# Mixer C of a hybrid encoder: its diagonal blocks moved by ScalarE's block copies, with four unread TensorE products for the first direction

## The chip, the cores and the metric

The kernel runs on one core of one Trainium2 chip. The metric is device time in microseconds (us), the median of several executions. The core's engines each run a queue of their own in order and wait for one another on semaphores: TensorE (PE, with its weight loads PEld), VectorE (DVE), ScalarE (ACT), GpSimd (POOL), and SyncE (SP), which issues most DMAs.

## What is computed

The reference is two encoder layers on 256 tokens of width 1024, in float32. Each layer projects the input once into the columns of four mixers, merges their gated outputs, and then applies a feed-forward block (layer 0) or a top-2-of-8 expert block (layer 1):

```python
for layer in range(DEPTH):                       # DEPTH = 2
    p = split_columns(x @ w_in[layer])
    y_a, y_b, y_c, y_d = mlstm(p), dilated_attention(p), deltanet_branch(p), window_attention(p)
    mix = (sum of sigmoid(gate_i) * (y_i @ w_branch_i)) @ w_out
    x = layer_norm(alpha * x + mix)
    x = layer_norm(alpha * x + (swiglu(x) or moe_swiglu(x)))
```

The change lies in mixer C, the gated DeltaNet, which runs over the sequence in both directions. For each direction and each chunk it solves a triangular system:

```python
decay = exp(where(incl, gc[i] - gc[j], -inf))
a_strict = where(strict, (k_beta @ k.T) * decay, 0.0)
sol = triangular_solve(a_strict, rhs, lower=True, unit_diagonal=True)
```

## The kernel before

A float32 product is done as three products of halves: ScalarE casts a weight to its high half (`wh<-raw`, L261), VectorE subtracts to get the low half (`wl<-raw,wh`, L264), and PE multiplies high by high, high by low and low by high into one PSUM bank. The names that PE's rows show for them are `mm<-wh,xh`, `mm<-wh,xl` and `mm<-wl,xh`. These projections of weight tiles are what PE does most of the time. In them the columns of a product are 256, 264 or 512.

In a layer's mixing stage the four mixers are generators. Between weight tiles `advance(n)` lets each of them emit a step, ahead of the projections' own instructions by a priority offset of 56. A list scheduler then orders each engine's queue by these priorities and by what is ready, so that taking an instruction out in one place moves others. Products of the mixers stand as `mx` in PE's rows, and each `mx` or `mm` tile is a bank from one of two rings of four.

Mixer C (`mix_c`) has two chunk pairs `t` and two directions `d`, 0 and 1. `systems(t)` computes the triangular systems `U` (tile `cU`, 128 partitions x 4 heads x 128). `leaves(d)` inverts their 32 x 32 diagonal blocks for one direction. It first gathers the blocks into `cYZ`: VectorE multiplies `U` by a block mask (`cum`, L132), adds up the four column groups (L878), copies the sum three more times (L880) and transposes it (L881). POOL starts `cX` as an identity. Then come 31 elimination steps on VectorE, two small instructions each (`cXt`, `cX`). The result is transposed to `cWc` (L900) and spread back over a block-diagonal tile `cW` by another masked multiply (L132), whose transpose is `cV` (L905). `unit(d, t)` combines the 32 x 32 blocks on PE, beginning with `mx<-cW,cU` products. `leaves` runs once for each direction in each of the two layers.

Rows of the sections below also name tiles of other mixers: `bp` (probabilities of mixer B's attention, evacuated by ScalarE), `bk` (its keys), `aw` (mixer A's weights) and `cS` (mixer C's state). `warm(n)` issues `n` products of an identity whose result nobody reads; the kernel before calls it outside the mixing stage.

Of the kernel before, what the change touches and what calls it, by code (L numbers as in the profile page):

```python
# [12 lines left out]
OP = mybir.AluOpType  # L13
AX = mybir.AxisListType
PSUM = bass.MemoryType.PSUM

P = 128
# [100 lines left out]
class Encoder:  # L118
# [41 lines left out]
        self.last_mm = self.nc.tensor.matmul(o, l, r, start=start, stop=stop, skip_group_check=True)  # L160
        return self.last_mm

    def warm(self, n):

        with self.tc.issue_after(self.last_mm.ins):
            o = self.bmm()
            for _ in range(n):
                self.mm(o[:], self.c["identb"], self.c["mbb"][:, :512])

# [573 lines left out]
    def mix_c(self):  # L743
        mp, nc, c = self.mp, self.nc, self.c
# [27 lines left out]
        after = mp.tile([P, 2, P], F32R, name="cafter")  # L772
# [3 lines left out]
        o = self.bmx()  # L776
# [14 lines left out]
        o = self.bmx()  # L791
# [8 lines left out]
        for k in (1, 0):  # L800
            o = self.bmx()
            for t in range(2):
                x = mp.tile([P, 4, 64], F32, name="crx", tag="t1", bufs=4)
# [6 lines left out]
        o = self.bmx()  # L810
# [7 lines left out]
        o = self.bmx()  # L818
# [15 lines left out]
        r3 = lambda x: x[:].rearrange("p (h i) -> p h i", i=P)  # L834
        U, at, V, W = {}, {}, {}, {}
# [31 lines left out]
        def leaves(d):  # L867


            yz = self.m8("cYZ")  # L870
            y, z = yz[:, :1024], yz[:, 1024:]
            yv = y.rearrange("p (i x t h) -> p i x t h", x=4, t=2, h=4)
            k32 = c["blk32"][:, None, :, None].to_broadcast([P, 4, 4, 32])
            for t in range(2):
                m = self.t2("cum", "cs")
                mv = m[:].rearrange("p (h k i) -> p h k i", k=4, i=32)
                self.tt(mv, U[d, t].rearrange("p h (k i) -> p h k i", i=32), k32, OP.mult)
                nc.vector.tensor_reduce(yv[:, :, 0, t, :].rearrange("p i h -> p h i"), mv.rearrange("p h k i -> p h i k"), AX.X, OP.add)  # L878
            y4 = y.rearrange("p (i x m) -> p i x m", x=4, m=8)
            nc.vector.tensor_copy(y4[:, :, 1:4], y4[:, :, 0:1].to_broadcast([P, 32, 3, 8]))  # L880
            nc.vector.transpose(z, y)  # L881
            zv = z.rearrange("p (i j) -> p i j", j=32)
            x = mp.tile([P, 8, 32], F32, name="cX", bufs=1)
            nc.gpsimd.tensor_copy(x[:], c["own32b"].rearrange("p (q r) -> p q r", q=8))
            tmp = mp.tile([P, 8, 32], F32, name="cXt", bufs=1)
            yield
            for n in range(31):
                i = 31 - n if d else n
                rows = slice(0, i) if d else slice(i + 1, 32)
                cs = slice(i // 4, 8) if d else slice(0, i // 4 + 1)  # L890
                sh = [P, cs.stop - cs.start, rows.stop - rows.start]
                f = zv[:, rows, i][:, None].to_broadcast(sh)
                pv = x[:, cs, i:i + 1].to_broadcast(sh)
                tv = tmp[:, cs, rows]
                self.tt(tv, f, pv, OP.mult)
                self.tt(x[:, cs, rows], x[:, cs, rows], tv, OP.subtract)
                if n % 3 == 2:
                    yield
            wc = mp.tile([P, 256], F32, name="cWc", bufs=1)
            nc.vector.transpose(wc[:], x[:].rearrange("p q r -> p (q r)"))  # L900
            wcv = wc[:].rearrange("p (c t h) -> p t h c", t=2, h=4)
            for t in range(2):
                w, vv = self.t2("cW", "cW"), self.t2("cV", "cV")
                self.tt(w[:].rearrange("p (h k c) -> p h k c", k=4, c=32), wcv[:, t][:, :, None, :].to_broadcast([P, 4, 4, 32]), k32, OP.mult)
                nc.vector.transpose(vv[:], w[:])  # L905
                W[d, t], V[d, t] = r3(w), r3(vv)
            yield
# [86 lines left out]
        for d in range(2):  # L994
            yield from leaves(d)
            both = [unit(d, t) for t in (d, 1 - d)]
            for _ in range(3):
                for q in both:
                    next(q)
                    yield  # L1000
# [683 lines left out]
```

## Time and profile before

| | |
|---|---|
| median of 3 timed runs | 1400.27 us (1399.23 to 1401.48) |
| the profiled execution | 1396.19 us, span of the trace 1394.3 us |
| mean granted TensorE clock | 0.988 of full speed |
| PE busy | 1334.3 us, 96% of the span |
| DVE busy | 1077.3 us, 77% |
| ACT busy | 744.8 us, 53% |
| POOL busy | 144.1 us, 10% |
| chain that ended last, by engine | PE 80%, DVE 12%, issue 3%, ACT 2%, DMA 2% |

The span is the profiled execution seen by the hardware profiler, from its first to its last instruction; the time of that execution is a little longer. A busy share says how long an engine was at work, not whether anybody waited for it. What an engine waited for is in the table of waits and in brackets behind a row of the timeline, where the idle time just before the row stands with the instruction that ended it. The granted clock is that of TensorE in the stretch, as a share of full speed; its two levels are 1.2 and 2.4 GHz.

### The profile page before, as it was taken

Reading aid. Unit: us, or ns where it says so; the run is one execution under the profiler, and the core shown is the slowest. Engines: PE = TensorE matmul, PEld = TensorE weight load, DVE = VectorE, ACT = ScalarE, POOL = GpSimd, SP = SyncE. Lnnn points to the kernel's source line nnn. Section 1 sums busy time; section 2 is a strip of 40 time slices with the busy share of each in tenths; the row PEclk is TensorE's granted clock in tenths of the full one; section 3 lists DMA queues with packets and bytes.
Section 4 is the critical chain, followed back from the end, with each engine's and each line's share of the span. In section 5 each row is a group of like instructions: output and inputs, shape, how many; then the busy total and the mean of one; then the engine's idle time right before and its main releaser. Section 6 shows DMA issues by size and latency. Waiting matters only on the chain.

```text
span 1394.3 us, 23092 instructions
## 1 busy us (share of the span) xinstructions
PE 1334.3 (96%) x8736; PEld 1152.2 (83%) x8740; DVE 1077.3 (77%) x1880; ACT 744.8 (53%) x1102; POOL 144.1 (10%) x118
## 2 busy tenths in 40 slices
PE   8999999999999999999989999998899999999994
PEld 7877879999789998887688899986777878877873
DVE  6979876775785554777888489579988888888887
ACT  5535443464364443354434446436777678676773
POOL 1000200023100000100020002220111111111110
PEclk9999999999999999999999999999999999999998
DMA  7632422595596563243252238744989989989981
GB/s 247 183 99 76 147 61 82 154 337 163 177 298 183 187 190 103 85 127 102 61 171 85 73 111 288 244 146 167 358 303 357 332 317 324 359 305 343 369 301 71
DMA packets 155751, 281.90 MB, mean 202 GB/s; under 512 B 11120, under 2 KB 58480, under 8 KB 155632
## 3 DMA queue, kind: packets, MB, share of 16 engines
q1 hardware_dynamic: 153136, 273.54, 58.8%
q10 hardware_dynamic: 1152, 4.19, 0.9%
q0 software_dynamic: 1344, 2.62, 0.5%
q8 instruction: 70, 1.15, 0.3%
q14 instruction: 49, 0.40, 0.1%
HBM read 276.65 MB, written 2.10 MB: 200 GB/s over the span
## 4 chain that ended last, share of the span: by engine, by line
PE 80%; DVE 12%; issue 3%; ACT 2%; DMA 2%; POOL 0%; DVEq 0%; ACTq 0%; SPq 0%; POOLq 0%
PE mm L160 66%; PE mx L160 10%; DVE wl L264 4%; PE mx L172 3%; ACT wh L261 1%; DMA raw<-w_in_in 1%; DVE cXt L132 1%; DVE x L140 1%; DVE cX L132 1%; DMA raw<-moe_w_in 1%; DVE cW L132 1%; POOL crh L852 0%; DVE bnm L541 0%; DVE cYZ L878 0%; DVE bst L1076 0%
## 5 line engine op out<-in xcount | busy, mean ns | idle before, releaser
L264 DVE TENSOR_TENSOR wl<-raw,wh 128x1024 fp32r<-128x1024 f32 (+3 forms) x515 | 611.9, 1216 | 143.8 <-ACT wh L261 129.9
L261 ACT CAST wh<-raw 128x1024 fp32r<-128x1024 f32 (+3 forms) x539 | 522.8, 1004 | 293.7 <-PE mm L160 234.6
L160 PE MATMUL mm<-wh,xh 128*128 128x512 f32 (+4 forms) x736 | 191.5, 369 | 4.0 <-ACT wh L261 3.0
L160 PE MATMUL mm<-wh,xl 128*128 128x512 f32 (+4 forms) x736 | 184.0, 365 | 0.0
L160 PE MATMUL mm<-wl,xh 128*128 128x512 f32 (+4 forms) x544 | 150.1, 368 | 7.1 <-DVE wl L264 7.0
L160 PEld LDWEIGHTS mm<-wh,xh 128*128 128x128 f32 x736 | 129.6, 190 | 27.2 <-ACT wh L261 5.8
L160 PE MATMUL mm<-xh,wh 128*128 128x256 f32 x960 | 141.7, 287 | 7.7 <-ACT wh L261 6.6
L160 PEld LDWEIGHTS mm<-wh,xl 128*128 128x128 f32 x736 | 130.6, 191 | 19.7 <-issue 1.2
L160 PE MATMUL mm<-xl,wh 128*128 128x256 f32 x960 | 141.0, 286 | 0.0
L160 PE MATMUL mm<-xh,wl 128*128 128x256 f32 x960 | 140.2, 286 | 0.0
L160 PEld LDWEIGHTS mm<-xh,wh 128*128 128x128 f32 x960 | 125.5, 192 | 9.6 <-ACT wh L261 6.6
L160 PEld LDWEIGHTS mm<-xl,wh 128*128 128x128 f32 x960 | 125.8, 192 | 1.1 <-issue 0.3
L160 PEld LDWEIGHTS mm<-xh,wl 128*128 128x128 f32 x960 | 125.1, 192 | 0.8 <-issue 0.2
L160 PEld LDWEIGHTS mm<-wl,xh 128*128 128x128 f32 x544 | 94.1, 190 | 24.7 <-DVE wl L264 10.6
L264 POOL TENSOR_TENSOR wl<-raw,wh 128x1024 fp32r<-128x1024 f32 (+1 forms) x24 | 61.1, 2546 | 368.5 <-ACT wh L261 333.4
L1054 POOL TENSOR_TENSOR mg<-mg,th 128x512 f32<-128x512 f32 x24 | 45.5, 1919 | 351.5 <-DVE th L140 351.5
L160 PE MATMUL mm<-wh,hth 128*128 128x512 f32 x176 | 56.6, 397 | 0.0
L160 PE MATMUL mm<-wl,xl 128*128 128x512 f32 (+1 forms) x192 | 56.2, 374 | 0.0
L160 PE MATMUL mm<-wl,hth 128*128 128x512 f32 x176 | 55.7, 395 | 0.0
L160 PE MATMUL mm<-wh,htl 128*128 128x512 f32 x176 | 55.6, 394 | 0.0
L160 PE MATMUL mm<-yT,wh 128*128 128x256 f32 x320 | 43.2, 284 | 0.0
L160 PEld LDWEIGHTS mm<-wl,xl 128*128 128x128 f32 x192 | 35.5, 188 | 5.7 <-DVE wl L264 0.2
(375 smaller groups left out, 1721.2 us busy)
## 6 DMA issues: line engine op xcount, KB each, us to landing
raw<-moe_w_in SPq DMA_DIRECT2D x215, 512.0 KB, 6.2
raw<-w_in_in SPq DMA_DIRECT2D x132, 512.0 KB, 4.1
raw<-ffn_w_in SPq DMA_DIRECT2D x66, 512.0 KB, 3.9
raw<-moe_w_in SPq DMA_DIRECT2D x64, 384.0 KB, 4.6
raw<-w_out_in SPq DMA_DIRECT2D x16, 512.0 KB, 4.0
raw<-w_branch_d_in SPq DMA_DIRECT2D x8, 512.0 KB, 5.8
raw<-w_in_in SPq DMA_DIRECT2D x8, 396.0 KB, 3.8
raw<-w_branch_b_in SPq DMA_DIRECT2D x4, 512.0 KB, 3.3
```

Of the source, the lines that this page charges most:

```text
L132: return self.nc.vector.tensor_tensor(o, x, y, op)
L140: return self.nc.vector.scalar_tensor_tensor(o, x, s, y, op0, op1)
L160: self.last_mm = self.nc.tensor.matmul(o, l, r, start=start, stop=stop, skip_group_check=True)
L172: return self.nc.tensor.transpose(o, x, self.c["ident"][:x.shape[0], :x.shape[0]] if ident is None else ident)
L261: self.nc.scalar.copy(h[:, :m * n], raw[:, :m * n])
L264: eng.tensor_sub(l[:, :m * n], raw[:, :m * n], h[:, :m * n])
L1054: self.nc.gpsimd.tensor_tensor(m, m, x, OP.add)
```

## The change

In `leaves`, ScalarE copies each diagonal block where VectorE multiplied by the mask. For each `t`, four copies of 32 partitions x 128 elements take the blocks out of `U` straight into `cYZ`, in place of two masked multiplies and two reductions for each direction; the copy of the sum (768 elements) goes to ScalarE too. On the way back POOL sets `cW` to zero and four copies of ScalarE place the blocks. In the second loop direction 1 takes `t = 1` first. For direction 0, four products of 128 x 512 in bf16 whose result nobody reads are put behind the transpose into `cWc` in program order, in a bank of the `mx` ring.

```diff
-    def warm(self, n):
-
-        with self.tc.issue_after(self.last_mm.ins):
-            o = self.bmm()
+    def warm(self, n, after=None):
+
+        with self.tc.issue_after((after or self.last_mm).ins):
+            o = self.bmx() if after else self.bmm()
             for _ in range(n):
                 self.mm(o[:], self.c["identb"], self.c["mbb"][:, :512])
...
-            k32 = c["blk32"][:, None, :, None].to_broadcast([P, 4, 4, 32])
+            parts = [slice(32 * k, 32 * k + 32) for k in range(4)]
             for t in range(2):
-                m = self.t2("cum", "cs")
-                mv = m[:].rearrange("p (h k i) -> p h k i", k=4, i=32)
-                self.tt(mv, U[d, t].rearrange("p h (k i) -> p h k i", i=32), k32, OP.mult)
-                nc.vector.tensor_reduce(yv[:, :, 0, t, :].rearrange("p i h -> p h i"), mv.rearrange("p h k i -> p h i k"), AX.X, OP.add)
+                for r in parts:
+                    nc.scalar.copy(yv[r, :, 0, t, :].rearrange("p i h -> p h i"), U[d, t][r, :, r])
             y4 = y.rearrange("p (i x m) -> p i x m", x=4, m=8)
-            nc.vector.tensor_copy(y4[:, :, 1:4], y4[:, :, 0:1].to_broadcast([P, 32, 3, 8]))
+            nc.scalar.copy(y4[:, :, 1:4], y4[:, :, 0:1].to_broadcast([P, 32, 3, 8]))
             nc.vector.transpose(z, y)
...
-            nc.vector.transpose(wc[:], x[:].rearrange("p q r -> p (q r)"))
+            turned = nc.vector.transpose(wc[:], x[:].rearrange("p q r -> p (q r)"))
+            if d == 0:
+                self.warm(4, turned)
             wcv = wc[:].rearrange("p (c t h) -> p t h c", t=2, h=4)
-            for t in range(2):
+            for t in (d, 1 - d):
                 w, vv = self.t2("cW", "cW"), self.t2("cV", "cV")
-                self.tt(w[:].rearrange("p (h k c) -> p h k c", k=4, c=32), wcv[:, t][:, :, None, :].to_broadcast([P, 4, 4, 32]), k32, OP.mult)
+                nc.gpsimd.memset(w[:], 0.0)
+                for r in parts:
+                    nc.scalar.copy(r3(w)[r, :, r], wcv[r, t])
                 nc.vector.transpose(vv[:], w[:])
```

How the queues change is seen at three places of layer 1. The first is VectorE's queue where the second direction's blocks are gathered; `c_163` is the pack of constants with the mask. Before:

```order
L878 TENSOR_REDUCE cYZ<-cum 128x4x32
L132 TENSOR_TENSOR cXt<-cYZ,cX 128x2x26
L132 TENSOR_TENSOR cum<-cU,c_163 128x512
L132 TENSOR_TENSOR cX<-cX,cXt 128x2x26
L878 TENSOR_REDUCE cYZ<-cum 128x4x32
L132 TENSOR_TENSOR cXt<-cYZ,cX 128x2x25
L880 COPY cYZ<-cYZ 128x32x24
L132 TENSOR_TENSOR cX<-cX,cXt 128x2x25
L881 STREAM_TRANSPOSE cYZ<-cYZ 128x1024
L132 TENSOR_TENSOR cXt<-cYZ,cX 128x2x24
L264 TENSOR_TENSOR wl<-raw,wh 128x1024
```

The same engine in the changed kernel, where the line of the transpose is now L879:

```order
L879 STREAM_TRANSPOSE cYZ<-cYZ 128x1024
L140 SCALAR_TENSOR_TENSOR dnm<-dnm,nsink 128x2
L264 TENSOR_TENSOR wl<-raw,wh 128x1024
L132 TENSOR_TENSOR cXt<-cYZ,cX 128x31
L132 TENSOR_TENSOR des<-dnm,small 128x2x2
L264 TENSOR_TENSOR wl<-raw,wh 128x1024
L132 TENSOR_TENSOR cX<-cX,cXt 128x31
L879 STREAM_TRANSPOSE cYZ<-cYZ 128x1024
```

The gathering is gone from the queue, and the second direction's transpose moved up to the first direction's first elimination step. The second place is PE's queue around the first direction's first `cW` products. Before, they stand inside the third group of low halves:

```order
L160 MATMUL mm<-wl,xh 128x264 x4
L160 MATMUL mm<-wh,xh 128x264 x4
L160 MATMUL mm<-wh,xl 128x264 x4
L160 MATMUL mm<-wl,xh 128x264
L160 MATMUL mx<-cW,cU 32x32 x8
L160 MATMUL mm<-wl,xh 128x264 x3
```

In the changed kernel the products of the first chunk pair come after the same kind of projections, and are split in two:

```order
L160 MATMUL mm<-wh,xl 128x264 x4
L160 MATMUL mm<-wl,xh 128x264 x4
L160 MATMUL mm<-wh,xh 128x264
L160 MATMUL mx<-cW,cU 32x32 x4
L160 MATMUL mm<-wh,xh 128x264 x3
L160 MATMUL mx<-cW,cU 32x32 x4
```

Counted over the program, 3609 `mm` products stand ahead of the first of them now, where 3665 did; in layer 0 it is 520 in place of 588. The third place is PE's queue where the unread products stand, in the changed kernel alone; `c_233` is the pack with the identity:

```order
L160 MATMUL mm<-wh,xl 128x512
L172 MATMUL mx<-c_163,ropeb 128x128
L160 LDWEIGHTS c_233
L160 MATMUL mx<-c_233 128x512
L160 LDWEIGHTS c_233
L160 MATMUL mx<-c_233 128x512
```

Two more such pairs follow. They stand among the projections of 512 columns, some 90 products ahead of the `cW` products in layer 1 and 46 in layer 0, and wait there for no other engine. In ScalarE's queue the eight copies into `cW` for the first direction stand in one row, between weight casts and evacuations of `bvn`; they wait for the transpose into `cWc`.

## Rows read from the trace of the kernel before

**Rows 1.** The page, part 1: busy time, share of the span and instructions.

```profile
PE 1334.3 (96%) x8736; PEld 1152.2 (83%) x8740; DVE 1077.3 (77%) x1880; ACT 744.8 (53%) x1102; POOL 144.1 (10%) x118
```

**Rows 2.** Windows: length, PE, PEld, DVE, ACT, POOL busy, PEclk, DMA share, GB/s.

```profile
90.00:260.00 170.00, 164.47 (x1373) 138.55 (x1374) 129.81 (x370) 76.73 (x174) 12.68 (x20) 0.99 0.29 87
660.00:870.00 210.00, 200.38 (x1671) 176.43 (x1670) 169.60 (x414) 97.54 (x183) 19.56 (x24) 0.99 0.41 128
```

**Rows 3.** PE's waits, 90 to 250 us: total, times, longest.

```profile
PE mx L172 <- ACT bp L143: 1.6, 2, 1.3
PE mx L160 <- DVE cW L132: 1.4, 1, 1.4
```

**Rows 4.** PE's waits, 650 to 850 us.

```profile
PE mx L160 <- DVE cW L132: 2.1, 2, 1.8
PE mm L160 <- DVE wl L264: 2.0, 1, 2.0
...
PE mx L172 <- ACT bp L143: 1.0, 2, 0.8
```

**Rows 5.** Windows: three short stretches.

```profile
213.00:221.00 8.00, 8.00 (x58) 7.62 (x57) 1.53 (x6) 1.51 (x4) 0.00 (x0) 0.79 0.00 0
690.00:700.00 10.00, 7.95 (x43) 6.53 (x42) 10.00 (x23) 2.75 (x10) 0.00 (x0) 1.00 0.04 6
...
721.00:726.00 5.00, 5.00 (x56) 4.70 (x57) 4.69 (x11) 3.46 (x6) 2.13 (x4) 0.66 0.52 163
```

**Rows 6.** DVE's timeline: start, us, instruction, count.

```profile
147.78 2.19 DVE L132 TENSOR_TENSOR cW<-cWc,c 128x512 f32<-128x512 f32 x2
...
695.34 0.54 DVE L880 COPY cYZ<-cYZ 128x768 f32<-128x768 f32 x1
...
697.20 1.21 DVE L264 TENSOR_TENSOR wl<-raw,wh 128x1024 fp32r<-128x1024 f32 x1
...
718.51 0.45 DVE L900 STREAM_TRANSPOSE cWc<-cX 128x256 f32<-128x256 f32 x1
...
719.19 2.22 DVE L132 TENSOR_TENSOR cW<-cWc,c 128x512 f32<-128x512 f32 x2
```

**Rows 7.** PE's timeline; in brackets the idle time before, and its releaser.

```profile
148.91 0.46 PE L160 MATMUL mx<-cW,cU 32*32 32x32 f32 x16 [1.43 <-DVE cW L132]
...
698.47 1.20 PE L160 MATMUL mm<-wl,xh 128*128 128x512 f32 x4 [2.05 <-DVE wl L264]
...
720.43 0.46 PE L160 MATMUL mx<-cW,cU 32*32 32x32 f32 x16 [1.80 <-DVE cW L132]
```

**Rows 8.** Groups by shape, DVE: count, busy us, mean ns, idle before.

```profile
L878 DVE TENSOR_REDUCE cYZ<-cum 128x128 f32<-128x512 f32 x8 | 8.6, 1077 | 0.0
L264 DVE TENSOR_TENSOR wl<-raw,wh 128x792 fp32r<-128x792 f32 x8 | 7.8, 978 | 0.8 <-PE mm L160 0.8
L132 DVE TENSOR_TENSOR cum<-cU,c 128x512 f32<-128x512 f32 x8 | 5.4, 680 | 0.0
...
L264 DVE TENSOR_TENSOR wl<-raw,wh 128x264 fp32r<-128x264 f32 x8 | 3.4, 423 | 0.0
```

**Rows 9.** PE's timeline: groups of products, the length of each with its tail.

```profile
142.88 0.64 PE L160 MATMUL mm<-wh,xl 128*128 128x264 f32 x4
143.36 0.64 PE L160 MATMUL mm<-wl,xh 128*128 128x264 f32 x4
...
944.34 1.03 PE L160 MATMUL mm<-c 128*128 128x512 bf16 x4
```

**Rows 10.** ACT: one row of its timeline, two groups by shape.

```profile
691.36 0.79 ACT L143 ACTIVATE bk<-mx 128x128 f32<-128x128 f32 x4 [1.23 <-PE mx L172]
...
L261 ACT CAST wh<-raw 128x768 fp32r<-128x768 f32 x64 | 50.8, 835 | 8.7 <-PE mm L160 8.6
...
L143 ACT ACTIVATE aw<-mx,aa 128x128 f32<-128x128 f32 x16 | 5.8, 364 | 3.8 <-PE mx L160 3.7
```

**Rows 11.** POOL: a group by shape.

```profile
L832 POOL MEMSET cS<- 128x256 f32 x4 | 1.1, 321 | 0.0
```

## The prediction

> **What bounds the kernel now.** I read the engine shares first. TensorE (PE) is busy 96% of a span of 1394.3 us and VectorE (DVE) 77% [rows 1]. So a DVE instruction is worth something only where PE stands still for it. The windows give the two stretches in which the diagonal blocks are worked on: 90 to 260 us in layer 0 and 660 to 870 us in layer 1 [rows 2]. In the first PE is idle 170 − 164.47 = 5.5 us, in the second 210 − 200.38 = 9.6 us; DVE is 76% and 81% busy there, ScalarE (ACT) 45% and 46%. 15.1 us is the ceiling on what idle time can give back.
>
> The table of PE's waits says for whom it stood still. In layer 0: 1.4 us once for cW and 1.6 us in two waits for bp [rows 3]. In layer 1: 2.0 us once for a low weight half (wl), 2.1 us in two waits for cW (the long one 1.8) and 1.0 for bp [rows 4]. The first long wait of layer 1 is explained by DVE's own timeline: DVE is busy without a gap from 690 to 700 us [rows 5], works on the second direction's blocks up to L880 and L881, and starts only at 697.20 the wl [rows 6] that PE has waited for since 698.47 − 2.05 = 696.4 [rows 7]. The long cW wait ends at 720.43 [rows 7]: the transpose into cWc starts at 718.51, and the two cW products run from 719.19 to 721.41 [rows 6]. Right behind it PE's granted clock is 0.66 over 721 to 726 us, the lower of its levels for part of the stretch [rows 5]; over these 5 us that costs 5 × (1 − 0.66) = 1.7 us.
>
> **The change part by part.** *Off DVE.* For each direction two cum (0.680) and two L878 (1.077) [rows 8], one L880 (0.54) and two cW (2.22) [rows 6]: 1.36 + 2.15 + 0.54 + 2.22 = 6.3 us, 25 us for the four directions. Nearly all of it is no gain by itself, because PE works meanwhile. Where it counts:
>
> (a) The wl wait. Of the 4.05 us per direction that go before the eliminations, the second direction's share stands immediately ahead of that wl. The need is 2.05 us [rows 7], so the wait goes whole: −2.05. What is late next is the low half behind it, one more 1.2 us of DVE later, while PE has eight products of 512 columns between two low halves: nothing is lost again.
>
> (b) The two cW waits. In layer 1 DVE turned cWc at 718.51 + 0.45 = 718.96 [rows 6]. Ahead of it go 2 × 4.05 = 8.1 us, and two wl of 792 and two of 264 columns (2 × 0.978 + 2 × 0.423 = 2.8 us [rows 8]) now stand behind it: about 708.0 if DVE is the limit until there. PE came at 720.43 − 1.80 = 718.63. It now finds 56 of the 264-column products fewer ahead of the cW product, at 0.12 us each (four per 0.48 us [rows 9]) 6.7 us, four unread products more, and wait (a) gone: 718.63 − 2.05 − 6.7 + 0.9 = 710.8. ScalarE's eight copies take 1.6 us if they run like the four bk evacuations that end after 0.79 us [rows 10], so cW is there at 709.6, 1.2 us ahead of PE. In layer 0 the same sum, with 68 products (8.2 us), gives PE at 148.91 − 1.43 − 8.2 + 0.9 = 140.2 [rows 7], and cW, counted back from its first product on DVE at 147.78, at about 147.8 − 10.9 + 1.6 = 138.5 [rows 6]. Both margins are thin, and DVE has some idle time that the shift cannot use, so I keep 0.4 us of wait in all: −(1.43 + 1.80 − 0.4) = −2.8. The bounds are −3.2 and, if DVE's idle time eats the shift, nothing.
>
> (c) The slow stretch at 721 to 726 goes with the wait before it: −1.7. That an idle time alone need not bring it shows at 698.47, where 2.05 us of idle left the clock at 1.00 [rows 5]; so it stays if other waits replace this one, and the bounds are 0 and −1.7.
>
> (d) The bp waits, 1.6 and 1.0 us, hang on ScalarE's turn behind DVE's results. I take −0.5 of 2.6; bounds −2.6 and +1.0, since ScalarE's queue also grows.
>
> *Onto ScalarE.* For each direction 16 copies of 32 partitions × 128 elements and one of 128 × 768. The trace has no 32-partition copy. The nearest rows are four bk evacuations of 128 elements in 0.79 us, 0.2 each, and the single aw of that size at 0.364; the 768 columns are priced by a cast of that size, 0.835 [rows 10]. So 16 × 0.2 + 0.84 = 4.0 us at the lower and 16 × 0.364 + 0.84 = 6.7 at the upper end for each direction, 16 to 27 us in all, against 206 us of ScalarE's idle time in the two stretches [rows 2]. I take the lower, since the eight copies stand in a row as the bk ones do. They are hidden by PE's weight products, but they stand ahead of weight casts and PSUM evacuations. I allow +0.6 for these.
>
> VectorE's page in the Trainium skill ("VectorE: DVE Perf Modes", the section on the TRN2 errata) says that ScalarE and VectorE pay a fixed latency for every instruction with an SBUF source, so that many small tiles pay it each time, and puts a 128-element copy on ScalarE at 350 cycles. By an estimate from that figure at 1.2 GHz a copy would be 0.29 us, the direction's bill 5.5 us and eight copies 2.3. The bk row above, which reads PSUM, is 0.2 start to start; no run here shows the SBUF form. By the page the margin in layer 1 shrinks from 1.2 to 0.5 us, which leaves the forecast.
>
> *Onto GpSimd (POOL).* Two memsets of 128 × 512 for each direction. A 128 × 256 one is 0.321 [rows 11], so 0.64 by length; POOL is 10% busy [rows 1], and the buffer was last read well before. Behind the later pairs stand the issues of bv's loads; 1.3 us of delay there is hidden by the products between. Cost 0, bounds 0 and +1.3.
>
> *Onto PE.* Four unread products of 128 × 512 in bf16 for the first direction of each layer. Four such run from 944.34 for 1.03 us with the tail of the last [rows 9]; start to start I estimate 0.22 each, 0.87 for four and 1.74 for both layers. They lie on the bounding engine in a stretch where it has work: +1.74, bounds 0 (if they fill an idle time) and +2.1. They carry no wait for the inverses, so they run when PE's queue reaches them, some 46 and 90 products ahead of the cW product. I therefore count no gain from them.
>
> *The rest.* The second t first for direction 1 costs nothing by itself: the same instructions. A reordered stretch brings small new waits: I allow +0.5, bounds −0.5 and +2.
>
> **The sum.** −2.05 − 2.8 − 1.7 − 0.5 + 0.6 + 1.74 + 0.5 = −4.2 us. The profiled execution took 1396.19 us for its span of 1394.3, so it would be 1392.0. That execution is 4.1 us below the median of the timed runs, 1400.27; on their scale, which I forecast, the result is 1396.1.
>
> **The rivals.** *ScalarE becomes the wait (slower).* The eight copies into cW stand at the head of its queue, waiting for cWc, with bvn evacuations and weight casts behind. For: PE's next weight products need those casts and free banks; ACT → PE waits already exist here (bp). Against: ScalarE is 45% busy. If a copy costs 0.364 the eight take 2.9 us; PE has four groups of products, some 2 us, before it needs the cast, waits 0.9, and so does the other direction. With (b) not gained, twice 1.8 us of new waits in the two layers and a slow stretch of 1.7 in each: −2.05 − 0.5 + 1.74 + 0.5 + 0.6 + 3.6 + 3.4 − 1.7 = +5.6, that is 1405.9. It decides from about 0.3 us a copy.
>
> *Waits only move (no change).* PE reaches the next late result (bp, or a later cW) as much earlier as it waited less. For: part of DVE's time returns as idle time, and bp's longest wait is 1.3 us in layer 0 [rows 3]. Against: wait (a) has a single cause. Then (a) and half of the cW waits are gained, −3.7, against +2.8 of costs; (c) stays: 1399.4.
>
> *More goes.* The slow stretch at 213 to 221 us in layer 0, clock 0.79 [rows 5], costs 8 × 0.21 = 1.7 us and lies behind layer 0's attention; if it and the bp waits (2.1 beyond (d)) go too: −8.0, 1392.3. Nothing in the change touches that place directly.
>
> *The unread products don't do what they are there for.* That holds in the forecast already: no gain is counted. If they did keep the clock up, it is term (c).
>
> **How the numbers follow.** Forecast (faster by about 4) 0.46, more goes 0.11, no change 0.26, slower through ScalarE 0.17. A difference under 0.2% of the median, 2.8 us, can't be told from none. The forecast's own range is 1393 to 1398.5, of which a fifth lies within 0.2%; so faster 0.11 + 0.38 = 0.49, within 0.08 + 0.26 = 0.32 (0.02 of it moved to slower), slower 0.19. The range for 8 in 10 runs from 1391.8 (more goes) to 1404, which leaves out the far half of the slower case.
>
> **What would show it.** Right: no PE wait for wl near 698 us and none over 0.5 us for cW in either layer; DVE's busy time down by about 25 us and ScalarE's up by 16 to 20; no granted clock near 0.5 behind layer 1's first cW product; the small copies at 0.2 us start to start. Wrong: PE waits for ScalarE (wh, bvn, cW) of more than 1 us in the two stretches; copies of 0.3 us or more; cW waits of the old length, which would mean that DVE isn't the limit of the eliminations; or a new slow stretch of the clock in either mixing stage.

## The result, and the profile after

The changed kernel took 1415.39 us, the median of four executions (1411.77 to 1418.92), where the kernel before took 1400.08 in the same comparison: a ratio of 1.0119, 95% interval 1.0099 to 1.0138. It is 15 us slower; the forecast was 4 us faster, and the time lies above the range. The profiled execution took 1418.92 us. (Ratios here compare executions within 1.5% of a kernel's fastest, which leaves out four of f2's ten, one of g4's and three of h2's; the experiments' medians are over all executions.)

The page of the changed kernel: its span, the busy times, and the granted clock in 40 equal slices, in tenths.

```profile
span 1417.1 us, 23183 instructions
...
PE 1357.1 (96%) x8742; PEld 1172.8 (83%) x8748; DVE 1058.9 (75%) x1852; ACT 775.0 (55%) x1170; POOL 149.0 (11%) x126
...
PEclk9999699999999999999978999999999999999998
```

Against [rows 1] DVE lost 18 us of work and ACT gained 30. PE is busy 23 us longer with the same products and the eight unread ones, and its idle time is the same 60.0 us as before. So the loss is not in waits at all. It is in the clock: the line has a 6 in slice 5 (142 to 177 us) and a 7 and an 8 around 730 us. The mean granted clock fell from 0.988 to 0.969. Time at full speed that was missing is (1 − 0.988) × 1394.3 = 16.7 us before and (1 − 0.969) × 1417.1 = 43.9 after: 27 us more, where the two spans differ by 22.8. All the rest of the change together gave some 4 us back. Span and mean clock were taken of each of the four executions: span times clock, the time at full speed, is 1373 us in every one of them, and 1378 in the profiled execution of the kernel before. So what the four scatter by is the clock too.

Where that time lies is seen in windows of 26 us that begin just ahead of the first direction's first `cW` product. First the kernel before, then the changed kernel, layer 0 and layer 1 each (length; PE, PEld, DVE, ACT and POOL busy with their counts; granted clock, DMA share, GB/s).

```profile
148.00:174.00 26.00, 24.85 (x260) 22.10 (x260) 21.25 (x71) 10.96 (x23) 4.74 (x8) 1.00 0.50 151
720.00:746.00 26.00, 25.41 (x254) 22.59 (x255) 20.60 (x73) 11.53 (x23) 2.13 (x4) 0.93 0.46 145
```

```profile
138.00:164.00 26.00, 24.96 (x179) 21.42 (x178) 11.44 (x38) 9.73 (x23) 6.07 (x12) 0.57 0.19 58
726.00:752.00 26.00, 25.83 (x182) 22.52 (x183) 11.12 (x37) 11.20 (x28) 6.04 (x12) 0.55 0.26 75
```

PE is busy 25 of 26 us in all four, yet the changed kernel gets through 180 products where the kernel before does 254 or 260. Its clock is at the lower level, 0.50, from 141.5 to 165.5 and from 728.5 to 752.5 us: 24 us each time, 12 us lost each time:

```profile
141.50:165.50 24.00, 23.71 (x156) 20.70 (x152) 10.53 (x36) 6.81 (x17) 6.75 (x14) 0.50 0.16 49
728.50:752.50 24.00, 24.00 (x160) 21.05 (x160) 10.31 (x37) 8.82 (x22) 5.13 (x10) 0.50 0.22 68
```

In the kernel before each of the six such stretches ahead of the last products lasts 3 to 3.5 us.

PE's waits in the two stages of the changed kernel, 90 to 250 and 650 to 850 us, which answer to [rows 3, 4]:

```profile
PE mx L172 <- ACT bp L143: 2.8, 3, 1.8
...
PE mx L160 <- ACT cW L906: 0.7, 1, 0.7
PE mm L160 <- ACT bvn L506: 0.3, 1, 0.3
...
PE mx L160 <- ACT cW L906: 2.2, 2, 1.8
PE mx L172 <- ACT dp L143: 1.1, 1, 1.1
...
PE mx L172 <- ACT bp L143: 0.5, 2, 0.3
```

The wait for wl is gone. The one for `cW` fell from 1.4 to 0.7 us in layer 0 and stayed in layer 1. New small ones stand for bvn and dp. (`bvn` holds mixer B's values, which ScalarE copies out of the bank of a projection; `dp` and, below, `ao` are other results that ScalarE evacuates.)

ScalarE's groups of the new work (count, busy us, mean ns, idle before), and the first of the rows of copies on its timeline:

```profile
L906 ACT COPY cW<-cWc 32x128 f32<-32x128 f32 x32 | 13.6, 426 | 5.1 <-DVE cWc L898 4.6
L876 ACT COPY cYZ<-cU 32x128 f32<-32x128 f32 x32 | 13.3, 415 | 1.2 <-DVE cU L140 0.9
L878 ACT COPY cYZ<-cYZ 128x768 f32<-128x768 f32 x4 | 3.3, 833 | 0.1
```

```profile
138.45 3.55 ACT L906 COPY cW<-cWc 32x128 f32<-32x128 f32 x8 [2.23 <-DVE cWc L898]
142.03 0.58 ACT L506 COPY bvn<-mm 128x512 f32<-128x512 f32 x1
```

A copy takes 0.42 us, eight in a row 3.55: twice the value taken for them, and above the upper bound of 0.364. PE's timeline over the same place shows what that does: the first products come with the first copies, the next eight 0.9 us later, and PE stands again, 0.29 us, for bvn, which ScalarE reaches only behind the copies. In layer 1 no such second pause follows: behind its wait of 1.76 us for `cW` PE waits for nothing over 0.1 us until the clock falls at 728.5.

```profile
138.92 0.43 PE L160 MATMUL mx<-cW,cU 32*32 32x32 f32 x8 [0.75 <-ACT cW L906]
139.29 0.62 PE L160 MATMUL mm<-wh,xl 128*128 128x256 f32 x3
139.84 0.43 PE L160 MATMUL mx<-cW,cU 32*32 32x32 f32 x8
...
142.66 0.81 PE L160 MATMUL mm<-wh,xh 128*128 128x264 f32 x2 [0.29 <-ACT bvn L506]
```

### The profile page after: what moved, and what is told of

Same layout as the page of the kernel before. It is cut to its first block, busy times and chain, and to the rows that moved or that the text cites. A ratio compares the mean times of both kernels' runs of the same rounds, so it can differ in the third digit from the quotient of the medians.

```text
span 1417.1 us, 23183 instructions
## 1 busy us (share of the span) xinstructions
PE 1357.1 (96%) x8742; PEld 1172.8 (83%) x8748; DVE 1058.9 (75%) x1852; ACT 775.0 (55%) x1170; POOL 149.0 (11%) x126
## 4 chain that ended last, share of the span: by engine, by line
PE 76%; DVE 12%; ACT 4%; DMA 3%; issue 3%; POOL 0%; SPq 0%; ACTq 0%; DVEq 0%; POOLq 0%
PE mm L160 62%; PE mx L160 11%; DVE wl L264 5%; PE mx L172 4%; ACT wh L261 2%; DMA raw<-w_in_in 1%; DMA raw<-moe_w_in 1%; DMA raw<-w_branch_a_in 1%; DVE cXt L132 1%; DVE x L140 1%; DVE cX L132 1%; DVE cacc L140 0%; ACT cYZ L876 0%; ACT cW L906 0%; DVE bnm L541 0%
## 5 line engine op out<-in xcount | busy, mean ns | idle before, releaser
L160 PE MATMUL mm<-wh,xh 128*128 128x512 f32 (+4 forms) x736 | 194.7, 374 | 3.3 <-ACT wh L261 3.0
L160 PE MATMUL mm<-wh,xl 128*128 128x512 f32 (+4 forms) x736 | 188.5, 370 | 0.0
L160 PE MATMUL mm<-wl,xh 128*128 128x512 f32 (+4 forms) x544 | 154.5, 375 | 5.1 <-DVE wl L264 5.0
```

## The experiments

The theory at the start (A): ScalarE's eight copies into `cW` bring the cW products late and thin out the large products around them, and there TensorE's clock falls and stays low. The rivals: the unread products (B), and the earlier place of the first direction's products in the queue, whoever copies (C).

The first four part the change: without the unread products (e1), with the spread into `cW` back on VectorE (e2), with the gathering back on VectorE (e3), and with the unread products tied to cWc (e4).

**e1**, without the unread products:

```diff
-            if d == 0:
-                self.warm(4, turned)
```

> The changed kernel without the four unread products; all else as in it. Theory A (ScalarE's eight copies into cW, 3.5 us in the trace, bring the cW products late and thin out the large products around them, and the clock falls there and stays low for 23 us in either layer): both slow stretches stay, granted clock 0.97, time 1410 to 1417. Rival B (the unread products, which run 8 to 19 us too early and push the queue, are the cause): both stretches gone, 1390 to 1396.

Measured: 1415.88 us, ratio to the kernel before 1.0129 (1.0086 to 1.0172). The unread products neither cause the loss nor cost 1.7 us that could be seen. A stretch of 24 us stands at 725.5 to 749.5, as in the changed kernel; the other one left the first direction of layer 0 (its clock there is 1.00) and came at the second, 189.5 to 213.5. Rival B is out.

**e2**, spread by VectorE:

```diff
-                nc.gpsimd.memset(w[:], 0.0)
-                for r in parts:
-                    nc.scalar.copy(r3(w)[r, :, r], wcv[r, t])
+                k32 = c["blk32"][:, None, :, None].to_broadcast([P, 4, 4, 32])
+                self.tt(w[:].rearrange("p (h k c) -> p h k c", k=4, c=32), wcv[:, t][:, :, None, :].to_broadcast([P, 4, 4, 32]), k32, OP.mult)
```

> The changed kernel with cW again by VectorE's masked multiply; gathering stays on ScalarE, the unread products stay. Theory A: no 23 us stretch at the low clock in either layer, 1391 to 1399. Rival C (it is the earlier place of the first direction's blocks among the projections, not who spreads them): both stretches stay, 1408 to 1416.

Measured: 1394.30 us, ratio 0.9981 (0.9954 to 1.0008). The 26 us windows of this kernel, layer 0 and layer 1:

```profile
140.00:166.00 26.00, 25.19 (x259) 22.12 (x259) 21.17 (x69) 11.58 (x29) 7.09 (x13) 1.00 0.33 100
714.00:740.00 26.00, 25.70 (x266) 23.02 (x266) 21.33 (x66) 11.70 (x27) 5.05 (x10) 1.00 0.52 151
```

No long stretch, and 21 us less than the changed kernel. The position of the first direction's products is nearly that of the changed kernel (mixed among the same projections, 523 and 3612 `mm` products ahead of it in place of 520 and 3609), so the earlier place does not bring the loss by itself, as rival C had it. The wait is instructive; PE's timeline of this kernel:

```profile
140.63 0.45 PE L160 MATMUL mx<-cW,cU 32*32 32x32 f32 x16 [1.14 <-DVE cW L132]
...
714.14 0.46 PE L160 MATMUL mx<-cW,cU 32*32 32x32 f32 x16 [2.05 <-DVE cW L132]
```

PE stands longer for `cW` here than in the changed kernel (0.75 and 1.76), and its clock holds. So idle time ahead of `cW` does not bring the fall by itself.

**e3**, gathering back on VectorE (cum, L878 and L880 as before, the spread on ScalarE):

```diff
-                for r in parts:
-                    nc.scalar.copy(yv[r, :, 0, t, :].rearrange("p i h -> p h i"), U[d, t][r, :, r])
+                self.tt(mv, U[d, t].rearrange("p h (k i) -> p h k i", i=32), k32, OP.mult)
...
-            nc.scalar.copy(y4[:, :, 1:4], y4[:, :, 0:1].to_broadcast([P, 32, 3, 8]))
+            nc.vector.tensor_copy(y4[:, :, 1:4], y4[:, :, 0:1].to_broadcast([P, 32, 3, 8]))
```

> The changed kernel with the gathering again on VectorE (cum, reduction, copy); the spread into cW stays on ScalarE. Theory A: the long slow stretch stays in both layers, 1410 to 1420, and the wait for wl near 698 us is back (+2). Rival C: the first direction's products stand later again in layer 1 (75 products of 264 columns ahead in place of 25), so the stretches go: 1396 to 1402.

Measured: 1413.59 us, ratio 1.0126 (1.0061 to 1.0192). The time is theory A's; the profiled execution has the long stretch in layer 0 alone (149.5 to 173.5), not in both. The first direction's products stand late again in both layers (576 and 3659 `mm` products ahead). In layer 0 the stretch came all the same, against rival C; in layer 1 it stayed away in this one execution, as C had it.

**e4**, the unread products reading cWc:

```diff
             if d == 0:
-                self.warm(4, turned)
+                o = self.bmx()
+                for _ in range(4):
+                    self.mm(o[:, :256], c["ident"], wc[:])
```

> The changed kernel with the four unread products reading cWc (float32, 256 columns), so that they run only once the first direction's inverses are turned. If idle time of TensorE before cW is what brings the clock down (a part of theory A), the waits of 0.75 and 1.8 us are filled and the stretches go: 1392 to 1400. If the thin mix of large products behind it is (the other part of A, and rival C): both stretches stay, 1410 to 1418.

Measured: 1415.50 us, ratio 1.0124 (1.0080 to 1.0168), with the long stretch in layer 1 and one of 3.5 us in layer 0. Nothing is gained, but the edit did not fill the idle time either. PE now stands for cWc ahead of the tied products, at least as long as it stood for `cW` in the changed kernel (0.75 and 1.76):

```profile
138.21 0.67 PE L160 MATMUL mx<-cWc,c 128*128 128x256 f32 x2 [1.13 <-DVE cWc L898]
...
718.89 1.99 PE L160 MATMUL mx<-cWc,c 128*128 128x256 f32 x8 [1.98 <-DVE cWc L898]
```

So this run does not test what the idle time does; that it is not enough by itself rests on e2.

The next four change one size each.

**f1**, twelve unread products behind the first `cV` products of each layer:

```diff
                 self.ts(Vv[lo[n], :, hi[n]], h32(o[lo[n]]), -1.0)
+            if d == t == 0:
+                self.warm(12, self.last_mm)
```

> The changed kernel with twelve unread bf16 products of 512 columns in each layer behind the first direction's first cV products, where the long slow stretch starts; they take the places of weight products between the small ones. Theory A2 (the clock falls where small products crowd behind the late cW, and stays low because the large products between the small ones are too thin there): the stretches of 23 us shrink to a few us or don't come; 5 us more work, so 1397 to 1406. Rival D (once down, the clock stays down for that long whatever the engine does): both stay, 1418 to 1426.

Measured: 1416.08 us, ratio 1.0112 (1.0069 to 1.0155); both stretches stay, 24 us each. The expectation of A2 failed. But the products did not come in one piece: they lie one to three at a time between the small ones, where weight products had been, so this tests more work in a thin mix and not a dense piece.

**f2**, four copies of 256 elements in place of eight of 128:

```diff
+            w2 = mp.tile([P, 2, 4, P], F32, name="cW", bufs=1)
+            for r in parts:
+                nc.scalar.copy(w2[r, :, :, r], wcv[r])
```

> The changed kernel with four copies of 32 partitions x 256 elements in place of eight of 128, into one tile for both chunk pairs. If ScalarE pays mostly for each instruction (0.43 us each for 128 elements in the trace), a copy takes some 0.5 and the four 2.1 in place of 3.5. Theory A (length of the spread on ScalarE brings the fall): the long stretches go, 1392 to 1399. If the cause is that the spread sits in ScalarE's queue at all: they stay, 1410 to 1418.

ScalarE's group of these copies:

```profile
L905 ACT COPY cW<-cWc 32x256 f32<-32x256 f32 x16 | 10.7, 669 | 4.0 <-DVE cWc L898 3.8
```

0.67 us each, 2.7 for the four: less saved than expected. Measured: median 1410.27 us of ten executions that scatter from 1395.31 to 1422.88; ratio 1.0035 (1.0003 to 1.0066). They lie at three levels: 1395 to 1400, 1406 to 1411, and four at 1422. The profiled one, of 1421.99 us, has both long stretches. That is what none, one and two stretches of 12 us would make. Only the profiled execution has a trace, but the mean clock of every one is on record: 0.980 to 0.988 at the first level, 0.973 to 0.980 at the second and 0.964 to 0.967 at 1422. Span times clock is 1369 to 1377 us in all ten, so the scatter is the clock's.

**f3**, the same eight block copies by VectorE:

```diff
-                    nc.scalar.copy(r3(w)[r, :, r], wcv[r, t])
+                    nc.vector.tensor_copy(r3(w)[r, :, r], wcv[r, t])
```

> The changed kernel with the same eight block copies into cW on VectorE, zeroing on GpSimd kept. Theory A: a VectorE copy of that size is short (about 0.2 us), cW comes early, no long slow stretch: 1390 to 1397. If block copies with their thin order of products (4 cW products, 2 or 3 large, 4 more) are the cause whoever does them: 1408 to 1416.

```profile
L906 DVE COPY cW<-cWc 32x128 f32<-32x128 f32 x32 | 9.4, 293 | 0.7
```

Measured: 1396.28 us, ratio 1.0007 (0.9973 to 1.0041), no long stretch in the profile; four of ten executions lie at 1403 to 1412. The order of products is as thin, and the last blocks come as late (4.0 us after the transpose in layer 0, 3.6 in the changed kernel), but that does much less harm when ScalarE isn't the one that copies.

**f4**, e2 without the four unread products (the spread by VectorE):

```diff
-            if d == 0:
-                self.warm(4, turned)
```

> Gathering on ScalarE, spread by VectorE's masked multiply, no unread products: what is left of the change is the gathering alone. By the sum, 1.7 us less than with the unread products: 1390 to 1395, the fastest. If the unread products help the clock, it is slower than with them: 1396 to 1402.

Measured: 1406.48 us, ratio 1.0062 (1.0031 to 1.0093). The profile has a stretch of 17 us in layer 1 (717.5 to 734.5), behind a wait of 2.5 us for `cW` and 11 large products in place of e2's 15. So ScalarE's copies into `cW` are not needed for a long stretch. Whether the products themselves help or only the order that they bring can't be told from this: the scheduler moved `cW` by 15 large products.

Three more ask what ScalarE's copies do.

**g1**, the changed kernel with eight unread products in one piece between the first `cW` products and the `cV` products:

```diff
+            if d == t == 0:
+                with self.tc.issue_after(self.last_mm.ins):
+                    o = self.bmx()
+                    with self.together():
+                        for _ in range(8):
+                            self.mm(o[:], c["identb"], c["mbb"][:, :512])
             for n, o in enumerate(banks):
                 nc.vector.tensor_copy(pv[hi[n]], h32(o[hi[n]]))
```

> The changed kernel with eight unread bf16 products of 512 columns in one piece in each layer, right behind the first direction's first cW products and ahead of its cV products; seven weight products move behind. In the kernel before 15 large products stand there, in the changed one 3 and 7. Theory A3 (the clock falls, and stays low, because too little large work follows the wait for cW before the small products come): the 24 us stretches go or shrink to 3.5 us, 1395 to 1402 with 3.5 us of products added. If the late cW alone is enough: both stretches stay, 1415 to 1421.

Measured: 1414.51 us, ratio 1.0138 (1.0093 to 1.0183), four executions from 1405 to 1422. The profiled one has no long stretch here (one of 3 us at 724), but lost time to stretches of 7 us elsewhere. By the times it is not cured: the two executions at 1419 and 1422 have mean clocks of 0.969 and 0.968, like the changed kernel's. A3 is not borne out.

**g4**, e2 with the eight copies of ScalarE kept, into a tile that nothing reads:

```diff
+                f = mp.tile([P, 512], F32, name="cF", bufs=1)
+                for r in parts:
+                    nc.scalar.copy(r3(f)[r, :, r], wcv[r, t])
                 nc.vector.transpose(vv[:], w[:])
```

> VectorE's masked multiply makes cW as in e2, and ScalarE still does the same eight copies for each direction, into a tile that nothing reads. TensorE's queue is the same as in e2 but for a few products. If ScalarE's load (its casts and evacuations held up for 3.5 us) brings the fall: stretches are back, 1408 to 1416. If it is that TensorE's own products depend on these copies (A3): no long stretch, 1391 to 1398, as e2.

Measured: median 1406.95 us, ten executions from 1391.31 to 1412.62, ratio 1.0043 (1.0008 to 1.0078). Nothing of TensorE's depends on these copies, and yet 13 us of e2's gain are gone. PE's timeline of this kernel in layer 0, and its windows:

```profile
138.82 0.45 PE L160 MATMUL mx<-cW,cU 32*32 32x32 f32 x16 [1.13 <-DVE cW L132]
...
141.80 0.39 PE L160 MATMUL mm<-wh,xh 128*128 128x264 f32 x1 [0.90 <-ACT bvn L506]
```

```profile
138.00:164.00 26.00, 24.28 (x185) 21.20 (x186) 13.12 (x40) 9.13 (x22) 5.17 (x9) 0.62 0.18 55
721.00:747.00 26.00, 24.91 (x259) 22.23 (x260) 21.36 (x63) 14.78 (x34) 5.86 (x10) 1.00 0.50 140
```

In layer 0 the copies hold up bvn, PE stands a second time 3 us behind the first, the small products follow, and from 144.0 the clock is low for 20 us. In layer 1, where PE waits only 0.15 us behind `cW`, it holds.

**g5**, f4 with the eight products of g1:

```diff
+            if d == t == 0:
+                with self.tc.issue_after(self.last_mm.ins):
...
+                            self.mm(o[:], c["identb"], c["mbb"][:, :512])
```

> Gathering on ScalarE, spread by VectorE, without the four early unread products, but with eight in one piece behind the first cW products of each layer. Its twin without the eight (f4) has a stretch of 17 us in layer 1. A3: the stretch goes, 1392 to 1398. If not: 1405 to 1412.

Measured: 1398.21 us, ratio 1.0000 (0.9985 to 1.0016), ten executions from 1394 to 1402, and 3.5 us where f4 had 17. Behind a `cW` from VectorE one dense piece does help, by 8 us net.

The last four follow up the hint of g4.

**h1**, the changed kernel with bvn's evacuations on VectorE:

```diff
-                self.nc.scalar.copy(x[:, :n], b)
+                self.nc.vector.tensor_copy(x[:, :n], b)
```

> The changed kernel with bvn's evacuations (six for each layer) on VectorE in place of ScalarE. Theory E (ScalarE's 3.5 us of copies hold up what stands behind them, bvn first, so that TensorE stands a second time right behind the wait for cW, and there the clock falls): no wait for bvn, the 24 us stretches go in some or all executions, 1394 to 1404. Theory L (the late second half of cW is enough): 1408 to 1418.

Measured: 1398.18 us, ratio 1.0000 (0.9982 to 1.0019), ten executions from 1394 to 1406. Its windows:

```profile
138.00:164.00 26.00, 24.88 (x255) 21.73 (x255) 19.89 (x64) 13.35 (x32) 7.79 (x15) 1.00 0.37 102
711.00:737.00 26.00, 25.56 (x259) 22.47 (x260) 20.21 (x63) 14.17 (x34) 6.08 (x11) 1.00 0.51 150
```

One kind of instruction taken off ScalarE's queue brings 17 us, with all of the change in place. Here too the scheduler answered: 16 large products lie between the first `cW` and the `cV` products of layer 0, where there were 10, and in layer 1 PE waits 0.38 us for `cW`, where it waited 1.76. So the run does not part the free queue of ScalarE from the order that came with it.

**h2**, g4 with the same edit:

```diff
-                self.nc.scalar.copy(x[:, :n], b)
+                self.nc.vector.tensor_copy(x[:, :n], b)
```

> As g4 (cW by VectorE, eight copies of ScalarE into a tile that nothing reads) but with bvn's evacuations on VectorE. g4 took 1407 with a stretch of 20 us behind a wait of 0.9 us for bvn. Theory E: that wait goes and with it the stretch, 1391 to 1398. If ScalarE's copies bring it in another way (casts, a port): 1403 to 1412.

Measured: median 1411.49 us, ten executions, nine of them from 1400 to 1425 and one at 1475.53 (mean clock 0.838, which nothing here explains); ratio 1.0058 (1.0033 to 1.0083), with stretches of 17 and 24 us. Theory E's expectation failed. In layer 0 the order has no weight product left between the stages of `unit`, and PE stands between them, the first time where the clock falls (145.5). In layer 1 the wait for bvn, now on VectorE, lies 6 us ahead of `cW`, and right behind `cW` PE stands for `ao`, which ScalarE reaches only behind its eight copies; the clock falls at 729.1:

```profile
145.60 1.11 PE L160 MATMUL mx<-cwf,cU 64*64 64x64 f32 x8 [0.46 <-ACT cwf L945]
...
147.18 0.47 PE L160 MATMUL mx<-cV,cpg 64*64 64x64 f32 x2 [0.46 <-ACT cpg L951]
...
728.42 0.51 PE L160 MATMUL mm<-wh,xh 128*128 128x264 f32 x2 [1.35 <-ACT ao L143]
```

So bvn is not the only way: layer 1 has the same hold-up with another tile, layer 0 has a different one. What stands is weaker, below.

**h3**, half of the blocks placed by VectorE (the first chunk pair taken), half by ScalarE:

```diff
                 for r in parts:
-                    nc.scalar.copy(r3(w)[r, :, r], wcv[r, t])
+                    if t == d:
+                        nc.vector.tensor_copy(r3(w)[r, :, r], wcv[r, t])
+                    else:
+                        nc.scalar.copy(r3(w)[r, :, r], wcv[r, t])
```

> The changed kernel with the blocks of the first chunk pair placed by VectorE and those of the second by ScalarE, beside each other. ScalarE is held for 1.8 us in place of 3.5 and all of cW is there after about 2 us. Theories E and L both: no long stretch or one in some executions, 1391 to 1400. If any copy of ScalarE into cW is enough: 1408 to 1418.

Measured: 1398.45 us, ratio 1.0000 (0.9971 to 1.0029), no long stretch in the profile, three of ten executions at 1406 to 1409.

**h4**, e2 again, with no edit of its own:

> The kernel of e2 again (gathering on ScalarE, spread by VectorE's masked multiply, unread products kept), now in five rounds, as the best version so far: 1391 to 1397, 0.1 to 0.5% below the kernel before. If its first runs were lucky in the clock: 1398 to 1406.

Measured: 1394.64 us, twelve executions from 1388.01 to 1404.79, ratio 0.9973 (0.9945 to 1.0002). The profiled execution, one of the longer at 1400.52, has a stretch of 17 us in layer 1: e2's clock is better on the average, not safe. The two profiles are of the same program, PE works through the same order of products in both, and ahead of this place it waits 2.05 us for `cW` in both; in e2's the clock held. So order and waits do not decide it alone. Gathering on ScalarE with the spread on VectorE is the best version run, 21 us faster than the changed kernel. Against the kernel before it is 4 us faster in both series by the medians, and both intervals reach past 1.

The clock over the 26 us windows, in one profiled execution each:

| kernel | spread by, its copies on ScalarE | median us | clock, layer 0 | clock, layer 1 |
|---|---|---|---|---|
| before | VectorE, none | 1400.08 | 1.00 | 0.93 |
| changed | ScalarE, 8 | 1415.39 | 0.57 | 0.55 |
| e1 | ScalarE, 8 | 1415.88 | 1.00 | 0.54 |
| e3 | ScalarE, 8 | 1413.59 | 0.54 | 1.00 |
| e4 | ScalarE, 8 | 1415.50 | 0.93 | 0.58 |
| f1 | ScalarE, 8 | 1416.08 | 0.57 | 0.55 |
| f2 | ScalarE, 4 longer | 1410.27 | 0.56 | 0.55 |
| g1 | ScalarE, 8, dense piece | 1414.51 | 1.00 | 0.93 |
| h1 | ScalarE, 8, bvn on VectorE | 1398.18 | 1.00 | 1.00 |
| h3 | both, 4 | 1398.45 | 1.00 | 1.00 |
| g4 | VectorE, 8 unread | 1406.95 | 0.62 | 1.00 |
| h2 | VectorE, 8 unread, bvn on VectorE | 1411.49 | 0.67 | 0.56 |
| e2, h4 | VectorE, none | 1394.30, 1394.64 | 1.00, 1.00 | 1.00, 0.67 |
| f3 | VectorE, none | 1396.28 | 1.00 | 1.00 |
| f4, g5 | VectorE, none | 1406.48, 1398.21 | 0.93, 1.00 | 0.67, 0.93 |

The windows are of one execution each; the mean clock of every execution is on record too. Its median over a kernel's executions is 0.967 to 0.976 for the changed kernel, e1, e3, e4, f1, f2, g1, g4 and h2, 0.977 for f4, and 0.983 to 0.987 for before, e2, f3, g5, h1, h3 and h4. The median of span times clock is 1367 to 1378 us in all of them, while the median times run from 1394 to 1416: what parts the longer from the shorter ones is the clock.

## Why the prediction was wrong

**What held.** The wl wait went whole, as in (a). Leaving the clock aside, the two profiled executions differ by 22.8 − 27.2, some −4 us; the sum without its term (c) was −2.5. e2 and h4, where the clock mostly holds, came out 4 us under the kernel before, which is the size of the sum, though not its kernel.

**The step that failed is (c), and the same price in the rival on ScalarE.** I took a slow stretch at the 1.7 us that one of 3.5 us costs, the only length that the trace of before shows ahead of the last products, gave back one such stretch, and let the rival add one in each layer. The changed kernel has a stretch of 24 us in each, 12 us apiece, and three of 7 us where the kernel before has 3.5: −1.7 became +27. The rival named the right engine and the right place: its eight copies ahead of the bvn evacuations were to make PE stand. But the 3.6 us of new waits that it counted did not come: PE stood once for bvn, 0.3 us, and its idle time is the same 60.0 us. Of its terms the slow stretches came, seven times as dear. With 12 us in place of 1.7 for each stretch it would have read +26 by its own sum, above what came. It had the chance 0.17 because ScalarE is 45% busy, an average that says nothing on 3.5 us in one piece at the place where PE needs it.

**The size of a copy was off.** 0.2 was taken from evacuations of PSUM by 128 partitions, with 0.364 as the upper end; it is 0.42. The copy of 768 elements over all partitions came at 0.833, as priced, so it is the small form that was off. ScalarE's bill is 30 us, not 16 to 27, and eight copies hold its queue for 3.55 us, over the point of about 0.3 us a copy at which the rival was to decide. The estimate from the Trainium skill ("VectorE: DVE Perf Modes", the section on the TRN2 errata), 0.29, was nearer than the row that I took, and still short; its rule that many small tiles pay the fixed part each time agrees with f2, where twice the elements cost 0.67 and not 0.84.

**Term (b) came to −0.6 in place of −2.8.** By the tables of waits 2.9 us for `cW` are left of 3.5. In layer 0 PE came at 138.2, where the sum had 140.2, and cWc was turned at 138.4, where it had 136.9 (138.5 less the copies' 1.6); in layer 1, later by the stretch in layer 0, they came at 724.4 and 725.7. The work taken off DVE did not move the transpose as far as the sum had it. As I read the trace, what is left on DVE in the 10 us ahead of it is little but the eliminations, which start 0.2 to 0.3 us apart and each read the result of the one before, and two or three low halves; there was little work left to take out from between them. That was my reservation, at the wrong size.

**Small terms.** The unread products cost 1.74 by the sum; e1, without them, is not faster by anything that its interval can show. (Its span times clock has a median of 1367 us against 1373, so a cost of that order may lie under the clock's scatter.) (d) went the other way in layer 0: bp 2.8 in place of 1.6 us. DVE's busy time fell by 18, not 25.

**What is shown and what stays open.** Shown: the loss is TensorE's lower clock in mixer C's units; the spread on ScalarE is the part of the change that brings it (e2 and f3 against the changed kernel, while e3, without the gathering, keeps the loss); ScalarE's copies do so in part even where nobody needs their result (g4, against e2, 13 us). The unread products do not bring it (e1), and the wait ahead of `cW` is not enough by itself (e2); whether it takes part no run settles, since e4 only moved it. A spread on ScalarE isn't the only way to a long stretch (f4, h4). Argued, but not shown: that the common part is a second pause or a thin mix of products right behind `cW`, on which the clock falls and then stays low while small products alternate with a few large ones. The pauses in g4's layer 0 and h2's layer 1, and h1, fit that. Against the pause stand the changed kernel's layer 1 and f1, which fell without one. Against the thin mix stand e2's layer 0 and layer 1 of h1 and h3, which held with 11, 10 and 9 large products between the first `cW` and the first `cV` products, where the changed kernel has 10. f1 and g1 don't settle it. Since each edit moved the order of TensorE's queue too, and the same program (e2, h4) fell in one profile and held in the other, the exact trigger is left open.

## What to carry to other kernels

Where small dependent products alternate with large ones, price a fall of TensorE's clock by the whole section in which it could stay low, and not by the shortest stretch that the trace of before happens to show. Before work goes to an engine that is half idle, look at what stands behind it in that engine's queue at that place: a row of eight copies is one block of 3.5 us for all that follows. A price per instruction must come from the same form: the row taken here differed in partition count and in source (PSUM, not SBUF), and was half the price; which of the two makes the difference no run shows.

## What the runs showed of the hardware

Copies of ScalarE from SBUF to SBUF with 32 partitions took 0.42 us at 128 elements and 0.67 at 256; VectorE's took 0.29 at 128; ScalarE's four evacuations of PSUM by 128 partitions at 128 elements take 0.79 us together. Ahead of the last products, stretches at TensorE's lower clock lasted 3 to 3.5, 6.5 to 7, 10, 17, 20 or 23.5 to 24 us in these traces. PE was busy nearly throughout (23.71 and 24.00 of 24 us in the changed kernel), and the same section of mixed small and large products ran at the full clock in e2's and h3's profiles. Executions of one program fell up to 28 us apart with the clock (f2: 1395 us at a mean of 0.988, 1423 at 0.965), and one profile of a program had a stretch of 17 us where another had none (h4, e2).
